# One chunk of the recurrent tail per step: reordering scans, square roots and first convolutions in a hybrid RG-LRU and attention kernel

## The chip, the cores and the metric

The kernel runs on one core of a Trainium2 chip. The metric is the device time of one execution in microseconds (us), the median of several runs; lower is better.

The engines are named as the profile names them: PE is TensorE's matrix multiply and PEld its weight load, DVE is VectorE, ACT is ScalarE, POOL is GpSimd, and SP is SyncE, whose queue issues nearly all transfers. Every engine works through its own queue strictly in order, so an instruction that waits holds everything behind it on the same engine.

## The reference

One layer of a hybrid decoder is computed for a prompt of 2048 tokens and for 64 sample tokens (8 sequences of 8): a recurrent branch, a dilated sliding-window attention over three groups of heads, and a gated merge of the two. The change touches the recurrent branch alone:

```
xa, ga = the first two blocks of 1024 columns of  rms_norm(x) @ w_in
xa = conv_b + sum(xa[t - 3 + j] * conv_w[j] for j in range(4))   # causal convolution
r  = sigmoid(xa @ w_a + b_a)       # block diagonal, 8 blocks of 128 channels
i  = sigmoid(xa @ w_x + b_x)
log_a = -8 * r * softplus(-lambda)
a  = exp(log_a)
u  = sqrt(-expm1(2 * log_a)) * (i * xa)
h[t] = a[t] * h[t-1] + u[t]        # the scan over time
out  = h * silu(ga)                # later multiplied by w_lru_proj
```

The kernel takes `-expm1(2 log_a)` as `(a*a + 1) * tanh(-log_a)`, so it needs a tanh, an exp, a square root and, for the gates and silu, sigmoids.

## The kernel before

All 2112 tokens (2048 of the prompt and 64 of the sample) lie along the free dimension, and the normalized, transposed input stays in SBUF as a high and a low part (`RH`, `RL`). Products are formed in three passes (high by high, high by low, low by high). The order of every engine is written out by hand (`tc.manual_schedule()`), so the program order of the Python code is the order on each engine's queue. The tokens are cut into five chunks, `CH`: 512, 512, 384, 384 and 320 tokens.

The program goes through attention and its gating, then the recurrent branch, which the change touches, then the merge gates (`gm_block`, with the sample attention planned into their steps), and then three output projections.

The recurrent branch loops over 8 blocks `b` of 128 channels. A block has two halves of five steps, one step a chunk:

- In the first half each step forms `xa` for one chunk with 24 matmuls (`zT`, L760) into a PSUM tile `zt` of which there are four, and `evac` (L861) copies it into `xpad`.
- In the second half each step forms `ga` for one chunk with 24 matmuls, puts silu of it into `sgl` (L961 on ACT, L962 on DVE), and then `gates_b` runs the six gate matmuls of that chunk (`zga`, L888), two sigmoids (`rr` L890, `ii` L892) and a product on POOL (L893). The gate matmuls read `xh`, the convolution's result split by `gates_a` into a high part (L879 on ACT) and a low part (L880 on DVE). `xh` is a single buffer. The third of the six gate matmuls is the first that reads the low part.
- `conv` for a chunk is an Identity on ACT (L868), then three multiply-adds on DVE (L870). It writes `xc`, which the tail of the block before still reads until its scan of that chunk is done.

What remains of a block after its gates, its tail, runs under the next block's matmuls: `tail_1` (tanh, L897), `tail_2` (exp on ACT L902, a square on POOL L904, a multiply-add on DVE L905), and `tail_3`: a square root on ACT (L910), a product (L911), the scan (L919) on DVE, the product with `sgl` on POOL (L920), and a store of `sgl` to `Y1` from SP's queue (L921). For block `b - 1` the steps of block `b` issue them so: `tail_1` in step 0, `tail_2` in step 1, `tail_3` of chunks 0 to 2 in step 2, `conv` of chunk 0 in step 3, and in step 4 `gates_a` of chunk 0, `tail_3` of chunks 3 and 4, and `conv` of chunk 1. In the second half step `ci` issues `gates_b` of chunk `ci`, `gates_a` of chunk `ci + 1` and `conv` of chunk `ci + 2`. Block 0 has no tail before it; block 7's tail runs in the first `gm_block`.

Of the kernel before, what the change touches and what calls it, by code (L numbers as in the profile page):

```python
# [13 lines left out]
AF = mybir.ActivationFunctionType  # L14
# [17 lines left out]
CH = ((0, 512), (512, 512), (1024, 384), (1408, 384), (1792, 320))  # L32
# [10 lines left out]
def program(tc, I, O, C, upto=99, debug=False):  # L43
# [7 lines left out]
    PE, ACT, DVE, POOL = nc.tensor, nc.scalar, nc.vector, nc.gpsimd  # L51
# [36 lines left out]
    def ztile(*tags):  # L88
        zi[0] += 1
        return ps.tile([128, 512], F32, name="zt", tag=tags[zi[0] % len(tags)])  # L90
# [6 lines left out]
    for g in (0, 1, 2):  # L97
        n = (WIN[g] - 8) * 1024
# [7 lines left out]
    def copy(n=1):  # L106
        for _ in range(n):
            if copies:
                i = dma(*copies.pop())
                if not G.manual:  # L110
                    tc.keep_in_program_order(i)
# [424 lines left out]
    for i in range(N + 3):  # L536
# [125 lines left out]
        if N - 4 < i < N:  # L662
            for k in range(3):
                if wbr:
                    n = min(wbr)
# [12 lines left out]
    def w_raw(src, nk=8):  # L678
        wr = wzp.tile([128, nk, 128], F32, name="wzr", tag="wzr")
        dma(wr, src)  # L680
        return wr

    def w_split(wr, eng, nk=8):
        w = wzp.tile([128, 2, nk, 128], F32R, name="wz", tag="wz", bufs=2)
        split(w[:, 0], w[:, 1], wr, eng)
        return w

    def wcols(c0):
        return win[:, c0:c0 + 128].rearrange("(k p) c -> p k c", p=128)
# [67 lines left out]
    def zT(z, w, c0, n):  # L757
        for i in range(24):
            k, p = divmod(i, 3)
            PE.matmul(z[:, 0:n], w[:, (0, 1, 0)[p], k, :], (RH, RH, RL)[p][:, k, c0:c0 + n], start=(i == 0), stop=(i == 23))  # L760
# [68 lines left out]
    def par_prep():  # L829
        prt = ps.tile([128, 8, 42], F32, name="prt", tag="tr")  # L830
        for n in range(8):
            PE.transpose(prt[:, n, :], rows[:, n * 128:(n + 1) * 128], ident[0:42, 0:42])
        DVE.tensor_copy(par, prt)
        DVE.tensor_scalar(e_, lam, -1.0, None, ALU.mult)
        DVE.tensor_tensor(e_, e_, lam, ALU.min)
        ACT.activation(e_, e_, AF.Exp)
        DVE.tensor_scalar(y_, e_, 2.0, None, ALU.add)
        DVE.reciprocal(y_, y_)
        DVE.tensor_mul(y_, y_, e_)
        DVE.tensor_mul(q_, y_, y_)  # L840
        DVE.tensor_scalar(c8, q_, 2.0 / 19, 2.0 / 17, ALU.mult, ALU.add)
        for i in (15, 13, 11, 9, 7, 5, 3, 1):
            DVE.tensor_mul(c8, c8, q_)
            DVE.tensor_scalar(c8, c8, 2.0 / i, None, ALU.add)
        DVE.tensor_mul(c8, c8, y_)
        DVE.tensor_scalar(e_, lam, -1.0, 0.0, ALU.mult, ALU.max)
        DVE.tensor_add(c8, c8, e_)
        DVE.tensor_scalar(n8, c8, 8.0, None, ALU.mult)
        DVE.tensor_scalar(c8, c8, -8.0, None, ALU.mult)
# [5 lines left out]
    tt = lp.tile([128, NT], F32, name="tt")  # L855
# [3 lines left out]
    def evac(c0, n, z):  # L859
        npr = min(n, SEQ - c0)  # L860
        ACT.copy(xpad[:, 3 + c0:3 + c0 + npr], z[:, 0:npr])  # L861
        if npr < n:
            ACT.copy(xsp[:, :, 3:11], z[:, npr:n].rearrange("p (s t) -> p s t", t=8))
# [13 lines left out]
    def gates_a(c0, n):  # L877
        xh = lp.tile([128, 2, 512], F32R, name="xh", tag="xh")
        ACT.copy(xh[:, 0, 0:n], xc[:, c0:c0 + n])  # L879
        DVE.tensor_sub(xh[:, 1, 0:n], xc[:, c0:c0 + n], xh[:, 0, 0:n].bitcast(F32))  # L880
        return xh
# [13 lines left out]
    def tail_1(b):  # L895
        for c0, n in CH:
            ACT.activation(tt[:, c0:c0 + n], rr[:, c0:c0 + n], AF.Tanh, scale=n8[:, b:b + 1])  # L897

    def tail_2(b):
        for c0, n in CH:  # L900
            s = slice(c0, c0 + n)
            ACT.activation(rr[:, s], rr[:, s], AF.Exp, scale=c8[:, b:b + 1])  # L902
            a2 = lp.tile([128, 512], F32, name="a2", tag="ii", bufs=2)
            POOL.tensor_mul(a2[:, 0:n], rr[:, s], rr[:, s])  # L904
            DVE.scalar_tensor_tensor(tt[:, s], a2[:, 0:n], 1.0, tt[:, s], ALU.add, ALU.mult)  # L905

    def tail_3(b, i0=0, i1=5):
        for c0, n in CH[i0:i1]:
            s = slice(c0, c0 + n)
            ACT.activation(tt[:, s], tt[:, s], AF.Sqrt)  # L910
            DVE.tensor_mul(xc[:, s], xc[:, s], tt[:, s])  # L911
            if c0 + n == NT:
                a0 = rr[:, SEQ:NT:8]
                hh = lp.tile([128, 8], F32, name="hh", tag="hh")
                DVE.tensor_mul(hh, a0, par[:, b, 34:42])
                DVE.tensor_add(xc[:, SEQ:NT:8], xc[:, SEQ:NT:8], hh)
                DVE.memset(a0, 0.0)
            init = 0.0 if c0 == 0 else tt[:, c0 - 1:c0]
            DVE.tensor_tensor_scan(tt[:, s], rr[:, s], xc[:, s], init, ALU.mult, ALU.add)  # L919
            POOL.tensor_mul(sgl[:, s], sgl[:, s], tt[:, s])  # L920
            dma(Y1[b][:, s], sgl[:, s])  # L921
        if i1 < 5:
            return
        POOL.tensor_copy(par[:, b, 4:5], tt[:, SEQ - 1:SEQ])
        POOL.tensor_copy(par[:, b, 34:42], tt[:, SEQ + 7:NT:8])

    for b in range(8):
        for ci, (c0, n) in enumerate(CH):
            z = early.pop(ci, None) if b == 0 else None
            if z is None:  # L930
                z = ztile("z", "S")
                zT(z, wx, c0, n)
            evac(c0, n, z)
            copy()
            if ci == 0:
                gr = lp.tile([128, 2, 128], F32, name="gr", tag="gr")
                dma(gr[:, 0], I["lru_w_a"][0, b])
                dma(gr[:, 1], I["lru_w_x"][0, b])
                wga = w_split(wgr, DVE)
                wxr = w_raw(wcols((b + 1) * 128 if b < 7 else C_GM))  # L940
            if b == 0 and ci == 2:
                par_prep()
            if b and ci < 3:
                (tail_1, tail_2, lambda b: tail_3(b, 0, 3))[ci](b - 1)
            if ci == 3:
                POOL.tensor_copy(xsp[:, :, 0:3], par[:, b, 10:34].rearrange("p (s j) -> p s j", j=3))
                gw_ = lp.tile([128, 2, 2, 128], F32R, name="gw_", tag="gw_")
                split(gw_[:, 0], gw_[:, 1], gr, DVE)
                conv(b, *CH[0])
            if ci == 4:  # L950
                xh = gates_a(*CH[0])
                if b:
                    tail_3(b - 1, 3, 5)
                conv(b, *CH[1])
        for ci, (c0, n) in enumerate(CH):
            z = ztile("z", "S")
            zT(z, wga, c0, n)
            if ci == 0:
                wx = w_split(wxr, DVE)
                wgr = w_raw(wcols(1024 + (b + 1) * 128 if b < 7 else C_GM + 128))  # L960
            ACT.activation(sgl[:, c0:c0 + n], z[:, 0:n], AF.Sigmoid)  # L961
            DVE.tensor_mul(sgl[:, c0:c0 + n], z[:, 0:n], sgl[:, c0:c0 + n])  # L962
            gates_b(b, c0, n, xh, gw_)
            if ci < 4:
                xh = gates_a(*CH[ci + 1])
            if ci < 3:
                conv(b, *CH[ci + 2])
            copy()
        POOL.tensor_copy(par[:, b, 0:3], xpad[:, SEQ:SEQ + 3])
        POOL.tensor_copy(par[:, b, 10:34].rearrange("p (s j) -> p s j", j=3), xsp[:, :, 8:11])  # L970
# [15 lines left out]
    def gm_block(f, w, hooks, gtile):  # L986
        for ci, (c0, n) in enumerate(CH):
            z = ztile("z", "S")
            zT(z, w, c0, n)
            for h in hooks.get(ci, ()):  # L990
                h()
            gt = gtile()
            ACT.activation(gt[:, 0:n], z[:, 0:n], AF.Sigmoid, bias=par[:, f % 8, 8 + f // 8:9 + f // 8])  # L993
            dma(Gsc[f][:, c0:c0 + n], gt[:, 0:n])  # L994
            copy()
            if plan and f:
                for fn in plan.pop(0):
                    fn()

    plan = []  # L1000
    wm = {0: wx}

    def nextw(f):
        if f + 1 < 16:
            wm[f + 1] = w_split(G.wr, DVE)

    def nextr(f):
        if f + 2 < 16:
            G.wr = w_raw(wcols(C_GM + (f + 2) * 128))

    G.wr = wgr
    gm_block(0, wm[0], {0: (lambda: nextw(0), lambda: nextr(0), lambda: tail_1(7), lambda: tail_2(7)), 1: (lambda: tail_3(7),), 4: (states,)},
             lambda: lp.tile([128, 512], F32, name="gt0", tag="ii", bufs=2))
    lr.close()
    gts = ExitStack()
# [387 lines left out]
    for c in range(8):  # L1403
        for f in range(8):
            n = c * 8 + f
# [51 lines left out]
    for c in range(8):  # L1457
        c0, n = TC[c]
# [128 lines left out]
```

## Time and profile before

| | |
|---|---|
| median of 3 runs | 2606.82 us (2605.22 to 2612.3) |
| the profiled execution's own time | 2603.89 us |
| its span, first to last instruction | 2602.1 us |
| mean granted TensorE clock | 0.988 of full speed |
| busy share of the span: DVE, ACT, POOL | 60%, 42%, 21% |

The busy share of an engine is an average over stages of different kinds; what a change within one stage can bring is read from that stage's own waits. A timeline row gives the start, the duration, the engine, the line, the operation, the tiles, and in brackets the idle time of the engine just before it and what ended that idle time.

### The profile page before, as it was taken

Reading aid. Unit: us, or ns where it says so; the run is one execution under the profiler, and the core shown is the slowest. Engines: PE = TensorE matmul, PEld = TensorE weight load, DVE = VectorE, ACT = ScalarE, POOL = GpSimd, SP = SyncE. Lnnn points to the kernel's source line nnn. Section 1 sums busy time; section 2 is a strip of 40 time slices with the busy share of each in tenths; the row PEclk is TensorE's granted clock in tenths of the full one; section 3 lists DMA queues with packets and bytes.
Section 4 is the critical chain, followed back from the end, with each engine's and each line's share of the span. In section 5 each row is a group of like instructions: output and inputs, shape, how many; then the busy total and the mean of one; then the engine's idle time right before and its main releaser. Section 6 shows DMA issues by size and latency. Waiting matters only on the chain. (4 is left out here: it accounts for less than half of the span.)

```text
span 2602.1 us, 44722 instructions
## 1 busy us (share of the span) xinstructions
PE 2512.8 (97%) x15196; PEld 2351.1 (90%) x15196; DVE 1553.9 (60%) x4805; ACT 1080.6 (42%) x3327; POOL 553.3 (21%) x897
## 2 busy tenths in 40 slices
PE   8999999999999999999999998999998999999999
PEld 7999999999999999999988887888887999998988
DVE  6744686777776777557555666655775723432322
ACT  5534453443453443444455545544556621211110
POOL 4422322221221221223223333320000002200000
PEclk9999999999999999999999999999999999999999
DMA  5443564555554343247533333346555569633332
GB/s 150 108 136 95 145 180 138 163 154 151 154 149 118 105 120 111 78 131 235 182 111 134 105 107 117 105 140 197 186 174 171 169 181 345 206 120 116 118 117 68
DMA packets 311289, 376.73 MB, mean 145 GB/s; under 512 B 54915, under 2 KB 254927, under 8 KB 308221
## 3 DMA queue, kind: packets, MB, share of 16 engines
q1 hardware_dynamic: 297028, 356.31, 44.4%
q0 software_dynamic: 14032, 17.57, 2.5%
q8 instruction: 120, 1.97, 0.3%
q14 instruction: 109, 0.89, 0.1%
HBM read 293.55 MB, written 168.31 MB: 177 GB/s over the span
## 5 line engine op out<-in xcount | busy, mean ns | idle before, releaser
L336 PE MATMUL z<-w,RH 128*128 128x384 f32 (+1 forms) x3088 | 889.2, 349 | 4.9 <-POOL w L317 2.4
L760 PE MATMUL zt<-RH,wz 128*128 128x384 f32 (+2 forms) x2560 | 705.9, 359 | 10.5 <-ACT gt L993 9.7
L336 PEld LDWEIGHTS z<-w,RH 128*128 128x128 f32 (+1 forms) x3088 | 553.3, 188 | 14.7 <-POOL w L317 6.5
L760 PEld LDWEIGHTS zt<-RH,wz 128*128 128x128 f32 x2560 | 471.2, 192 | 57.2 <-ACT gt L993 11.0
L336 PE MATMUL z<-w,RL 128*128 128x384 f32 x1544 | 520.3, 337 | 0.1
L760 PE MATMUL zt<-RL,wz 128*128 128x384 f32 (+2 forms) x1280 | 456.8, 357 | 0.0
L336 PEld LDWEIGHTS z<-w,RL 128*128 128x128 f32 x1544 | 291.5, 189 | 0.7 <-DVE RL L94 0.5
L178 DVE CUSTOM_DVE_ANT_0 kjk<-kt,qs 128x128 bf16<-128x128 f32 x768 | 228.1, 297 | 67.5 <-DMA SA<-Dsc 20.4
L760 PEld LDWEIGHTS zt<-RL,wz 128*128 128x128 f32 x1280 | 244.7, 191 | 23.0
L408 ACT ACTIVATE P<-P,o 128x128 f32<-128x128 f32 (+1 forms) x192 | 88.9, 463 | 311.1 <-DVE o L407 311.1
L345 ACT ACTIVATE jk<-z 128x128 bf16<-128x128 f32 (+1 forms) x408 | 113.0, 277 | 237.0 <-PE trc L376 173.6
L94 DVE TENSOR_TENSOR KQ<-trc,KQ 128x256 fp32r<-128x256 f32 x192 | 81.4, 424 | 208.7 <-ACT KQ L93 208.7
L347 POOL TENSOR_SCALAR ss<-ss 128x2 f32<-128x2 f32 (+1 forms) x204 | 44.5, 218 | 714.2 <-ACT jk L345 679.4
L1465 PEld LDWEIGHTS zt<-y1t,w_wlo 128*128 128x128 f32 x1536 | 190.3, 191 | 0.6
L1465 PE MATMUL zt<-y1t,w_wlo 128*128 128x256 f32 (+1 forms) x1536 | 190.6, 286 | 0.0
L1497 PE MATMUL zt<-w_wo,mt 128*128 128x512 f32 x672 | 162.0, 395 | 0.0
L1497 PEld LDWEIGHTS zt<-w_wo,mt 128*128 128x128 f32 x672 | 126.0, 188 | 30.7
L348 POOL TENSOR_TENSOR rs<-ss,neghalf 128x2 f32<-128x2 f32 (+1 forms) x204 | 142.6, 699 | 17.0
L1150 ACT ACTIVATE v<-v,P 128x128 f32<-128x128 f32 x256 | 81.1, 391 | 76.4 <-DMA v<-in_cache_kv_w 60.7
L434 DVE TENSOR_REDUCE o<-op 128x128 f32<-128x256 f32 x192 | 80.6, 420 | 44.9 <-PE op L429 44.8
L1499 DVE TENSOR_TENSOR xr<-zt,xr 128x512 f32<-128x512 f32 (+1 forms) x34 | 23.5, 692 | 137.3 <-PE zt L1497 132.6
L93 ACT CAST mt<-g 128x256 fp32r<-128x256 f32 x72 | 27.1, 388 | 187.2 <-DVE g L1468 172.1
(292 smaller groups left out, 4273.3 us busy)
## 6 DMA issues: line engine op xcount, KB each, us to landing
out_kv_s<-in_cache_kv_w SPq DMA_DIRECT2D x176, 480.0 KB
xt<-in_x_prompt SPq DMA_DIRECT2D x48, 512.0 KB
wr<-in_w_in SPq DMA_DIRECT2D x96, 192.0 KB
kt<-in_cache_kv_w SPq DMA_DIRECT2D x128, 128.0 KB
wzr<-in_w_in SPq DMA_DIRECT2D x32, 512.0 KB
v<-in_cache_kv_w SPq DMA_DIRECT2D x128, 128.0 KB
Osc<-o SPq DMA_DIRECT2D x192, 65.0 KB
ot<-Osc SPq DMA_DIRECT2D x32, 390.0 KB
```

The source lines that it names most:

```text
L94: eng.tensor_sub(l, src, h.bitcast(F32))
L178: DVE.tensor_tensor_reduce(jk, kts[q.tile][:, c], qts[t][:, c], 1.0, 0.0, ALU.mult, ALU.add, q.SC[:, o:o + 1])
L336: PE.matmul(u.z[0:m, :], (RH, RL, RH)[p][:, k, u.cols], Wt[(u.g, u.h), k][:, (0, 0, 1)[p], :], start=(i == 0), stop=(i == 23))
L345: ACT.activation(jk[0:m, :], z[0:m, i * 128:(i + 1) * 128], AF.Square, accum_out=u.ss[0:m, i:i + 1])
L347: POOL.tensor_scalar(u.ss[0:m, :], u.ss[0:m, :], 1.0 / HD, EPS, ALU.mult, ALU.add)
L348: POOL.tensor_tensor(u.rs[0:m, :], u.ss[0:m, :], neghalf[0:m, :], ALU.pow)
L408: ACT.activation(u.P[:, 0:n], u.P[:, 0:n], AF.Exp, bias=u.o[:, 128:129], scale=-1.0, accum_out=u.o[:, 129:130])
L434: DVE.tensor_reduce(u.o[:, 0:128], u.op.rearrange("p a b -> p b a"), AX.X, ALU.add)
L760: PE.matmul(z[:, 0:n], w[:, (0, 1, 0)[p], k, :], (RH, RH, RL)[p][:, k, c0:c0 + n], start=(i == 0), stop=(i == 23))
L1150: ACT.activation(v2s[n][:, h], v2s[n][:, h], AF.Copy, scale=P2[:, h, n:n + 1])
L1465: PE.matmul(z[:, 0:n], wl[k][:, (0, 1, 0)[p], f, :], y1s[c * 8 + k][:, (0, 0, 1)[p], 0:n], start=(i == 0), stop=(i == 23))
L1497: PE.matmul(z[0:m, :], ms_[k][:, (0, 0, 384)[p] + o:(0, 0, 384)[p] + o + m], wo[k][:, (0, 1, 0)[p], e * 4:(e + 1) * 4, :].rearrange("p k c ...
```

## The change

The square roots leave `tail_3` for a step of their own, `tail_r`, all five in step 2 of the first half. `tail_3` then handles one chunk in each of five steps: chunks 0, 1 and 2 in steps 2, 3 and 4 of the first half, chunks 3 and 4 in steps 0 and 1 of the second. The new block's `conv` of chunk 0 and the split of its gate weights move from step 3 to step 2, behind the scan of chunk 0; `gates_a` of chunk 0 and `conv` of chunk 1 move from step 4 to step 3, behind the scan of chunk 1. Nothing is added to or taken from what is computed.

```
--- before.py
+++ after.py
@@ -904,10 +904,13 @@
             POOL.tensor_mul(a2[:, 0:n], rr[:, s], rr[:, s])
             DVE.scalar_tensor_tensor(tt[:, s], a2[:, 0:n], 1.0, tt[:, s], ALU.add, ALU.mult)
 
+    def tail_r(b):
+        for c0, n in CH:
+            ACT.activation(tt[:, c0:c0 + n], tt[:, c0:c0 + n], AF.Sqrt)
+
     def tail_3(b, i0=0, i1=5):
         for c0, n in CH[i0:i1]:
             s = slice(c0, c0 + n)
-            ACT.activation(tt[:, s], tt[:, s], AF.Sqrt)
             DVE.tensor_mul(xc[:, s], xc[:, s], tt[:, s])
             if c0 + n == NT:
                 a0 = rr[:, SEQ:NT:8]
@@ -941,16 +944,16 @@
             if b == 0 and ci == 2:
                 par_prep()
             if b and ci < 3:
-                (tail_1, tail_2, lambda b: tail_3(b, 0, 3))[ci](b - 1)
-            if ci == 3:
+                (tail_1, tail_2, tail_r)[ci](b - 1)
+            if b and ci > 1:
+                tail_3(b - 1, ci - 2, ci - 1)
+            if ci == 2:
                 POOL.tensor_copy(xsp[:, :, 0:3], par[:, b, 10:34].rearrange("p (s j) -> p s j", j=3))
                 gw_ = lp.tile([128, 2, 2, 128], F32R, name="gw_", tag="gw_")
                 split(gw_[:, 0], gw_[:, 1], gr, DVE)
                 conv(b, *CH[0])
-            if ci == 4:
+            if ci == 3:
                 xh = gates_a(*CH[0])
-                if b:
-                    tail_3(b - 1, 3, 5)
                 conv(b, *CH[1])
         for ci, (c0, n) in enumerate(CH):
             z = ztile("z", "S")
@@ -963,6 +966,8 @@
             gates_b(b, c0, n, xh, gw_)
             if ci < 4:
                 xh = gates_a(*CH[ci + 1])
+            if b and ci < 2:
+                tail_3(b - 1, ci + 3, ci + 4)
             if ci < 3:
                 conv(b, *CH[ci + 2])
             copy()
@@ -1009,7 +1014,7 @@
             G.wr = w_raw(wcols(C_GM + (f + 2) * 128))
 
     G.wr = wgr
-    gm_block(0, wm[0], {0: (lambda: nextw(0), lambda: nextr(0), lambda: tail_1(7), lambda: tail_2(7)), 1: (lambda: tail_3(7),), 4: (states,)},
+    gm_block(0, wm[0], {0: (lambda: nextw(0), lambda: nextr(0), lambda: tail_1(7), lambda: tail_2(7)), 1: (lambda: tail_r(7), lambda: tail_3(7),), 4: (states,)},
              lambda: lp.tile([128, 512], F32, name="gt0", tag="ii", bufs=2))
     lr.close()
     gts = ExitStack()
```

## Rows read from the trace of the kernel before

**Rows 1.** Page, part 1: busy time, share of the span, instructions.

```profile
PE 2512.8 (97%) x15196; PEld 2351.1 (90%) x15196; DVE 1553.9 (60%) x4805; ACT 1080.6 (42%) x3327; POOL 553.3 (21%) x897
```

**Rows 2.** PE's waits, recurrent branch: total us, times, longest.

```profile
PE zga L888 <- ACT xh L879: 22.5, 7, 3.2
PE zga L888 <- DVE xh L880: 8.4, 7, 1.8
```

**Rows 3.** Timeline of PE, blocks 1 and 2.

```profile
1329.92 2.36 PE L888 MATMUL zga<-xh,gw__17935 128*128 128x512 f32 x6 [3.21 <-ACT xh L879]
...
1356.59 0.63 PE L760 MATMUL zt<-RH,wz 128*128 128x512 f32 x2
...
1384.71 0.40 PE L760 MATMUL zt<-RL,wz 128*128 128x512 f32 x1
1388.32 2.67 PE L888 MATMUL zga<-xh,gw__18385 128*128 128x512 f32 x6 [3.21 <-ACT xh L879]
...
1399.14 1.19 PE L888 MATMUL zga<-xh,gw__18385 128*128 128x512 f32 x4 [1.36 <-DVE xh L880]
```

**Rows 4.** Timeline of PE, second half of block 0, start of block 1.

```profile
1274.99 1.56 PE L888 MATMUL zga<-xh,gw__17501 128*128 128x512 f32 x6
...
1292.76 1.21 PE L888 MATMUL zga<-xh,gw__17501 128*128 128x384 f32 x6
...
1298.20 0.63 PE L760 MATMUL zt<-RH,wz 128*128 128x512 f32 x2
```

**Rows 5.** Windows, block 2: length, five engines' busy us, PEclk, DMA share, GB/s.

```profile
1388.00:1390.00 2.00, 1.68 (x5) 1.06 (x6) 1.67 (x3) 2.00 (x5) 0.00 (x0) 0.81 0.64 261
1390.00:1392.00 2.00, 2.00 (x6) 1.58 (x5) 1.97 (x5) 1.98 (x2) 1.16 (x1) 0.50 0.00 0
...
1398.00:1400.00 2.00, 0.86 (x4) 0.73 (x5) 1.96 (x4) 0.33 (x1) 0.00 (x0) 1.00 0.39 111
```

**Rows 6.** Timeline of DVE, block 2.

```profile
1377.84 1.23 DVE L919 TENSOR_TENSOR_SCAN tt<-rr,xc 128x512 f32<-128x512 f32 x1
...
1379.69 2.21 DVE L919 TENSOR_TENSOR_SCAN tt<-rr,tt,xc 128x512 f32<-128x512 f32 x1
...
1384.55 3.06 DVE L870 SCALAR_TENSOR_TENSOR xc<-xpad,par,xc 128x512 f32<-128x512 f32 x3
1388.30 0.69 DVE L880 TENSOR_TENSOR xh<-xc,xh 128x512 fp32r<-128x512 f32 x1 [0.68 <-ACT xh L879]
1388.90 0.55 DVE L911 TENSOR_TENSOR xc<-xc,tt 128x384 f32<-128x384 f32 x1
1389.49 1.02 DVE L919 TENSOR_TENSOR_SCAN tt<-rr,tt,xc 128x384 f32<-128x384 f32 x1
...
1395.56 2.32 DVE L94 TENSOR_TENSOR wz<-wzr,wz 128x1024 fp32r<-128x1024 f32 x1
...
1402.77 1.91 DVE L870 SCALAR_TENSOR_TENSOR xc<-xpad,par,xc 128x384 f32<-128x384 f32 x3
```

**Rows 7.** Timeline of ACT, block 2.

```profile
1379.10 0.82 ACT L868 ACTIVATE xc<-xpad,par 128x512 f32<-128x512 f32 x1 [2.21 <-DVE tt L919]
...
1387.65 0.62 ACT L879 CAST xh<-xc 128x512 fp32r<-128x512 f32 x1 [7.35 <-DVE xc L870]
```

**Rows 8.** Timeline of POOL, block 2.

```profile
1379.15 1.66 POOL L920 TENSOR_TENSOR sgl<-sgl,tt 128x512 f32<-128x512 f32 x1 [2.47 <-DVE tt L919]
...
1401.14 1.29 POOL L893 TENSOR_TENSOR xc<-xc,ii 128x512 f32<-128x512 f32 x1 [4.33 <-ACT ii L892]
```

**Rows 9.** POOL's product at line 893, all blocks: duration ns min/median/max.

```profile
L893 POOL TENSOR_TENSOR xc<-xc,ii x40: 881/1018/1816, 1278.1 to 1707.9; 128x512 f32<-128x512 f32 x16, 128x384 f32<-128x384 f32 x16, 128x320 f32<-128x320 f32 x8
```

**Rows 10.** Groups of DVE by form, block 0: busy us, mean ns, idle before.

```profile
L870 DVE SCALAR_TENSOR_TENSOR xc<-xpad,par,xc 128x512 f32<-128x512 f32 x6 | 4.5, 751 | 0.2
```

**Rows 11.** Groups of ACT, whole span: busy us, mean ns, idle before.

```profile
L910 ACT ACT_TABLE_LOAD x8 | 10.3, 1283 | 0.1
```

**Rows 12.** Transfers that touch Y1 or Y2, whole span.

```profile
DMA to landing us min/median/max: 3.2/6.2/12.6
```

More of the change, by code (lines that the diff above doesn't have):

```diff
@@ L905, in tail_2, with tail_r @@
             DVE.scalar_tensor_tensor(tt[:, s], a2[:, 0:n], 1.0, tt[:, s], ALU.add, ALU.mult)
+    def tail_r(b):
+        for c0, n in CH:
+            ACT.activation(tt[:, c0:c0 + n], tt[:, c0:c0 + n], AF.Sqrt)
     def tail_3(b, i0=0, i1=5):
@@ L909, in tail_3 @@
             s = slice(c0, c0 + n)
-            ACT.activation(tt[:, s], tt[:, s], AF.Sqrt)
             DVE.tensor_mul(xc[:, s], xc[:, s], tt[:, s])
@@ L943, in program @@
             if b and ci < 3:
-                (tail_1, tail_2, lambda b: tail_3(b, 0, 3))[ci](b - 1)
-            if ci == 3:
+                (tail_1, tail_2, tail_r)[ci](b - 1)
+            if b and ci > 1:
+                tail_3(b - 1, ci - 2, ci - 1)
+            if ci == 2:
                 POOL.tensor_copy(xsp[:, :, 0:3], par[:, b, 10:34].rearrange("p (s j) -> p s j", j=3))
@@ L949, in program @@
                 conv(b, *CH[0])
-            if ci == 4:
+            if ci == 3:
                 xh = gates_a(*CH[0])
-                if b:
-                    tail_3(b - 1, 3, 5)
                 conv(b, *CH[1])
@@ L965, in program @@
                 xh = gates_a(*CH[ci + 1])
+            if b and ci < 2:
+                tail_3(b - 1, ci + 3, ci + 4)
             if ci < 3:
@@ L1011, in program @@
     G.wr = wgr
-    gm_block(0, wm[0], {0: (lambda: nextw(0), lambda: nextr(0), lambda: tail_1(7), lambda: tail_2(7)), 1: (lambda: tail_3(7),), 4: (states,)},
+    gm_block(0, wm[0], {0: (lambda: nextw(0), lambda: nextr(0), lambda: tail_1(7), lambda: tail_2(7)), 1: (lambda: tail_r(7), lambda: tail_3(7),), 4: (states,)},
              lambda: lp.tile([128, 512], F32, name="gt0", tag="ii", bufs=2))
```

## The prediction

> **What bounds the kernel now.** I read the page first: PE is busy for 97% of the span [rows 1], so little but PE's own idle time and its slow clock can be won, and work saved on ACT, DVE or POOL is worth nothing by itself. The next view is the waits of PE alone, over the recurrent branch. It has two large rows, both at the gate matmuls, both seven times: 22.5 us for the high part of `xh` and 8.4 us for the low part [rows 2]. Seven is the number of blocks that run a tail of a block before them (1 to 7).
>
> The timeline of PE then gives one block. The gates of block 1 start at 1329.92 and those of block 2 at 1388.32, a period of 58.40 us. PE finishes the first `ga` chunk at 1384.71 + 0.40 = 1385.11, stands for 3.21 us, and in the next step stands again for 1.36 us for the low part [rows 3]. Block 0, which has no tail beside it, shows the pace without these waits: from its first gate matmul to the next block's first matmul 1298.20 - 1274.99 = 23.21 us [rows 4], against 1356.59 - 1329.92 = 26.67 us in block 1 [rows 3]. From a block's first matmul to its first gates PE needs 1385.11 - 1356.59 = 28.52 us. An unhindered block would so take 28.52 + 23.21 = 51.73 us, and 58.40 - 51.73 = 6.67 us are lost in each of seven blocks, 46.7 us in all.
>
> Where the loss beyond the two idle times comes from is in the windows. After the long wait the granted clock is 0.81 and then 0.50 in two windows of 2 us, half of 2.4 GHz; around the second wait of 1.36 us it stays at 1.00 [rows 5]. The long wait is paid a second time by the clock behind it, the short one isn't.
>
> Why the long wait is there is read on DVE and ACT. ACT waits 7.35 us for the convolution before it can cast `xh` [rows 7], because on DVE the convolution of chunk 0 (1384.55) stands behind three scans of the old block [rows 6]. The Identity that begins it had been done since 1379.92 [rows 7].
>
> **The change part by part.** Times are from here on counted from the block's first matmul (1356.59 in block 2).
>
> *Square roots together.* Five follow each other in step 2, before 3 in one place and 2 in another. The trace has 8 table loads of 1283 ns at that line for 8 tails [rows 11], one a tail already, so no load goes. Two roots of about half a us each move ahead of the Identity of chunk 0, which waits for the scan of chunk 0 anyway: nothing.
>
> *Convolution of chunk 0 behind the first scan.* The scan ends at 1379.07, or 22.5 [rows 6]. The Identity takes 0.82 [rows 7], the three multiply-adds 2.25 uncontended (3 x 751 ns [rows 10]) or 3.06 beside a POOL product [rows 6]; POOL's product with `sgl` starts just there, so I take 3.06: the convolution is done at 26.4, the high part of `xh` (0.62 [rows 7]) at 27.05. PE comes for it at 28.52. The long wait goes, and with it the slow clock. The low part stands in DVE's queue behind the product and scan of chunk 1: about 0.7 (0.55 for 384 tokens, made longer by 512/384), then 1.23 if POOL is free (the first scan) or 2.21 beside POOL's product [rows 6, 8]. POOL has long finished by then, so 1.23; then 0.69. Following instructions overlap by some 0.09 (1388.30 + 0.69 against 1388.90 [rows 6]), so it is there at 28.85, and PE wants it two matmuls after 28.52, at 28.98. No wait, with 0.1 us to spare; with the scan at 2.21 it would be 0.85.
>
> *Evacuations behind the waiting Identities.* ACT's copies of chunks 3 and 4 now stand behind Identities that wait for scans (to about 23.3 and 29). Four `zt` tiles cover them: the matmuls that need these two back begin at about 37 and 42. Nothing, and some 12 us of lateness would be covered.
>
> *The second half.* Here the removed work is late next. In before, DVE ran without a pause from 1388.90 to 1402.77 + 1.91 = 1404.68, 15.78 us, for the rest of the tail, two convolutions and a part of the third, a weight split and three splits of `xh` [rows 6]. All of it stays between the first low part and the convolution that the fourth chunk's gates need, and the product and scan of chunk 2 come in: 0.55 + 1.02 = 1.57 [rows 6]. DVE also waits for the Identity of chunk 1, which waits for its scan: about 0.3. And POOL's products with `sgl` of chunks 1 and 2 now fall here, 1.29 + 1.02 [rows 8, 9]. How much of a POOL product DVE loses lies between nothing and all of it; the scan beside a 1.29 us product lost 0.98, the convolution 0.81 beside a smaller one [rows 6, 8 to 10], and nothing is lost while DVE itself waits for ACT. I take two thirds, 1.5. Sum: 15.78 + 1.57 + 0.3 + 1.5 = 19.15. The convolution for the fourth chunk ends at 28.85 + 19.15 = 48.0, and the low part of its `xh` about 1.0 later, at 49.0. PE without waits gets there at 28.52 + (1292.76 - 1274.99) = 46.29 [rows 4], and wants the low part 0.35 later, 46.64. PE waits 49.0 - 46.6 = 2.4 us in all, spread over the gates of the second to fourth chunk in pieces of about 1 us, like the one of 1.36 that left the clock at 1.00 [rows 3, 5]. Behind the fourth chunk DVE has time again.
>
> The Trainium skill, "SBUF — State Buffer", section "Who interferes with whom", states that a VectorE instruction with two SBUF inputs and a GpSimd one that reads SBUF exclude each other, and that the one issued first holds the other for its whole length. By it the two thirds would be the whole wherever they meet, the second rival below; the scan at 2.21 beside 1.23 agrees with it, and 15.78 us of DVE beside four such products neither show nor deny it.
>
> *The sum.* 6.67 - 2.4 = 4.3 us in each of seven blocks, 30 us. Nothing takes it back: the order is written by hand, what follows starts when PE gets there, and block 7's tail in the first `gm_block` issues the same instructions in the same order on each engine. The profiled execution would go from 2603.89 to 2574; it lay 2.9 below the median of the runs, so the median goes from 2606.8 to 2577.
>
> **Bounds of the second half.** Four POOL products lie in the stretch already (chunks 3 and 4 of `sgl`, chunks 0 and 1 of `xc`): 1.02 + 0.88 + 2 x 1.29 = 4.5 us [rows 8, 9], of which by the same two thirds 3.0 are in the 15.78. Below: no POOL product costs DVE anything. Then 15.78 - 3.0 + 1.87 = 14.65 is early enough for every gate, all 46.7 us are won, and the time is 2560. Above: every POOL product in the stretch is paid in full. The new ones cost 2.3 instead of 1.5, the old ones 1.5 more: 21.45, a wait of 4.7, 2.0 us a block won, 2593.
>
> **The rivals.**
> 1. *All waits go* (2560 to 2568). For it: block 0's pace [rows 4], and DVE is busy for only 60% of the span [rows 1]. Against it: DVE had no pause in the stretch that gets longer.
> 2. *DVE takes the place of ACT's wait in full*: POOL and DVE exclude each other, and the gates wait 4 to 5 us a block for low parts, up to the bound above or a little beyond. At 5 that is 6.67 - 5 = 1.7 us a block, 12 us, about 2595. For it: scan and convolution [rows 6, 8]. Against it: the convolution lost less than a whole product [rows 6, 9, 10], and the times at which DVE waits for ACT let POOL through.
> 3. *It does nothing* (2600 to 2612): as in 2, and the pieces come together in one long wait at the third or fourth gates, so that the clock falls again (26.67 - 23.21 - 1.36 = 2.1 us a block with all that goes with it).
> 4. *Slower, by the stores.* Each chunk of `sgl` is overwritten by the new block's sigmoid (L961, on ACT) once its store has landed. The store of chunk 1 is now issued at about 30.3 and its overwriting is due when PE ends the second `ga` chunk, at about 35.5: 5 us. Stores and loads of these tensors took 3.2 to 12.6 us to land [rows 12]. ACT has about 2 us before `xh` for the third gates is late, so up to 7 us nothing happens; at 12.6 PE waits over 5 us at the third gates and the clock falls: 5.3 + 1.1 + 2.1 = 8.5 lost for 6.67, 2619. It decides from a landing of about 11 us. Against it: the range is mostly that of loads four times as large, and nothing else is queued at that moment but one copy.
>
> **How the numbers follow.** Within 0.3% (8 us) a measurement can't tell a change from none. Forecast, 2568 to 2586: 0.53. All waits go: 0.15. DVE in full, 2586 to 2599: 0.21. Nothing: 0.06. Slower: 0.05. Faster by over 0.3% is the first three, 0.89; same 0.06; slower 0.05. The range reaches from 2562 into the third case, to 2595, and leaves out the bare end of the second, the top of the third and the last two, some 0.2 together. All cases but the last two have one sign, so one range serves.
>
> **What would show it.** In the profile after: no wait of 3 us for L879 at `zga`; a granted clock of 1.00 through the branch; a period of about 54 us between the first gates of blocks; waits for L880, or short ones for L879, of 1 to 3 us a block at the second to fourth chunk; scans of 512 tokens at 1.2 us and not 2.2; still one table load per tail at L910; DVE without a pause for about 19 us behind the first low part. The forecast is wrong if the waits at the later gates sum to over 4 us or to under 1, if the clock still falls, or if ACT's sigmoid at L961 waits for a transfer.

## The result, and the profile after

| | before | changed |
|---|---|---|
| median | 2608.60 us (2605.22 to 2612.3, 4 runs) | 2572.27 us (2570.03 to 2578.51, 4 runs) |
| profiled execution, its span | 2603.89, 2602.1 | 2570.03, 2568.3 |
| ratio, 95% interval | | 0.9872, 0.9857 to 0.9886 |

The changed kernel is 36 us faster by the medians and 33.9 by the profiled executions. The forecast was 2577, with a range of 2562 to 2595.

The waits of PE over the recurrent branch of the changed kernel answer to [rows 2]. Beside two single waits at the branch's ends, which both kernels have, one row is left of the two at the gate matmuls. It has the same seven blocks, 1.2 us each instead of 3.2.

```profile
PE zga L888 <- ACT xh L879: 8.5, 7, 1.2
PE hp L982 <- POOL par L928: 5.4, 1, 5.4
```

The gate matmuls line by line show when the gates of block 1 and of block 7 start: (1647.1 - 1325.3) / 6 = 53.6 us a block, where it was 58.40 [rows 3].

```profile
L888 PE MATMUL zga<-xh,gw__17902 x30: 307/350/499, 1325.3 to 1350.4; 128*128 128x512 f32 x12, 128*128 128x384 f32 x12, 128*128 128x320 f32 x6
...
L888 PE MATMUL zga<-xh,gw__20602 x30: 307/352/503, 1647.1 to 1672.1; 128*128 128x512 f32 x12, 128*128 128x384 f32 x12, 128*128 128x320 f32 x6
```

Seven blocks at 58.40 - 53.63 = 4.77 us make 33.4 of the 33.9 us between the two profiled executions. The timeline of PE in block 2, which starts at 1350.58, answers to [rows 3, 4]: the first gates follow at once, the second are a little drawn out (six matmuls in 1.80 instead of 1.57), the third wait 1.22 us (the row shows the first four of their six matmuls).

```profile
1350.58 0.62 PE L760 MATMUL zt<-RH,wz 128*128 128x512 f32 x2
...
1378.93 1.57 PE L888 MATMUL zga<-xh,gw__18352 128*128 128x512 f32 x6
...
1385.93 1.80 PE L888 MATMUL zga<-xh,gw__18352 128*128 128x512 f32 x6
1393.12 1.21 PE L888 MATMUL zga<-xh,gw__18352 128*128 128x384 f32 x4 [1.22 <-ACT xh L879]
...
1398.68 1.41 PE L888 MATMUL zga<-xh,gw__18352 128*128 128x384 f32 x6
```

In the windows of 2 us the granted clock is 1.00 everywhere in the block, at the third gates too, where [rows 5] had 0.81 and 0.50 behind the long wait.

```profile
1390.00:1392.00 2.00, 1.90 (x11) 1.58 (x10) 1.96 (x2) 0.00 (x0) 2.00 (x2) 1.00 0.28 98
1392.00:1394.00 2.00, 0.88 (x4) 0.58 (x4) 1.97 (x5) 1.44 (x3) 0.06 (x1) 1.00 0.83 246
1394.00:1396.00 2.00, 2.00 (x13) 2.00 (x13) 1.90 (x7) 1.22 (x3) 0.62 (x1) 1.00 0.00 0
```

DVE's timeline in the same block answers to [rows 6]. The convolution of chunk 0 starts behind one scan, 5.0 us before the first gates of the block; the scan of chunk 1 takes 1.28 and not 2.21. What grew is the product of chunk 3, 1.64 where it took 0.55, and the convolution of chunk 2, 3.45 where it took 1.92.

```profile
1371.83 1.22 DVE L922 TENSOR_TENSOR_SCAN tt<-rr,xc 128x512 f32<-128x512 f32 x1
...
1373.94 2.71 DVE L870 SCALAR_TENSOR_TENSOR xc<-xpad,par,xc 128x512 f32<-128x512 f32 x3 [0.57 <-ACT xc L868]
...
1377.29 1.28 DVE L922 TENSOR_TENSOR_SCAN tt<-rr,tt,xc 128x512 f32<-128x512 f32 x1
1378.49 0.67 DVE L880 TENSOR_TENSOR xh<-xc,xh 128x512 fp32r<-128x512 f32 x1
...
1383.86 1.20 DVE L94 TENSOR_TENSOR wz<-wzr,wz 128x1024 fp32r<-128x1024 f32 x1
...
1386.41 1.64 DVE L914 TENSOR_TENSOR xc<-xc,tt 128x384 f32<-128x384 f32 x1
...
1389.03 3.45 DVE L870 SCALAR_TENSOR_TENSOR xc<-xpad,par,xc 128x384 f32<-128x384 f32 x3
...
1395.21 2.40 DVE L870 SCALAR_TENSOR_TENSOR xc<-xpad,par,xc 128x384 f32<-128x384 f32 x3
```

POOL's timeline has a product beside each of the two; e2 below shows that those of line 893 cost 2.0 us of it.

```profile
1384.03 1.92 POOL L923 TENSOR_TENSOR sgl<-sgl,tt 128x384 f32<-128x384 f32 x1 [3.72 <-DVE tt L922]
1385.90 1.74 POOL L893 TENSOR_TENSOR xc<-xc,ii 128x512 f32<-128x512 f32 x1
1389.19 1.31 POOL L923 TENSOR_TENSOR sgl<-sgl,tt 128x384 f32<-128x384 f32 x1 [1.55 <-DVE tt L922]
1390.46 1.60 POOL L893 TENSOR_TENSOR xc<-xc,ii 128x512 f32<-128x512 f32 x1
```

### The profile page after: what moved, and what is told of

It reads as the page before. It is cut to its first block, busy times and chain, and to the rows that moved or that the text cites. A ratio compares the mean times of both kernels' runs of the same rounds, so it can differ in the third digit from the quotient of the medians.

```text
span 2568.3 us, 44715 instructions
## 1 busy us (share of the span) xinstructions
PE 2501.8 (97%) x15196; PEld 2341.9 (91%) x15196; DVE 1541.6 (60%) x4805; ACT 1082.9 (42%) x3327; POOL 561.5 (22%) x897
## 3 DMA queue, kind: packets, MB, share of 16 engines
q8 instruction: 120, 1.97, 0.3%
```

## The experiments

Two questions were open. What are the 53.6 - 51.7 = 1.9 us a block that are still lost, and which part of the change, and of the loss before it, is worth what? Medians below are of 4 or more runs each; ratios are against the kernel before, run beside them. The intervals of e1 to e4 and of e6 overlap that of the changed kernel (0.9857 to 0.9886), so for a difference from it the traces speak: from the first gates of block 1 to those of block 7 the period is 53.6 us a block in the changed kernel, 53.45 in e1, 53.05 in e2 and e3, and 54.9 in e4 and e6.

**e1, the convolution ahead of the scan.**

```
             gates_b(b, c0, n, xh, gw_)
             if ci < 4:
                 xh = gates_a(*CH[ci + 1])
-            if b and ci < 2:
-                tail_3(b - 1, ci + 3, ci + 4)
             if ci < 3:
                 conv(b, *CH[ci + 2])
+            if b and ci < 2:
+                tail_3(b - 1, ci + 3, ci + 4)
```

> Changed kernel, but in the second half each step's convolution stands ahead of the scan instead of behind it. Theory (the 1.9 us a block that are left come from DVE's queue ahead of the third and fourth gates): product and scan of chunk 3 leave the way of the third gates, those of chunk 4 the way of the fourth; the wait of 1.2 us for the high part goes, the period falls from 53.6 to about 52.3 us, the time from 2572 to about 2563. Rival (DVE's whole work in the stretch counts, whatever its order): the wait moves to the fourth gates, time within 4 us of 2572.

Measured: 2571.28 us, ratio 0.9861 (0.9846 to 0.9877). The wait for the high part is gone, as the theory had it, but the time hardly moved: the rival was nearer. The split of the low part stands behind the same convolution and scan in DVE's queue, so the gates from the second chunk on now each wait a little for it: in PE's timeline of block 2 the third and fourth gates pause at their third matmul, and the fifth are drawn out to 1.38 from 1.04.

```profile
1388.79 0.51 PE L888 MATMUL zga<-xh,gw__18352 128*128 128x384 f32 x2
1389.49 0.96 PE L888 MATMUL zga<-xh,gw__18352 128*128 128x384 f32 x4 [0.20 <-DVE xh L880]
1394.46 0.51 PE L888 MATMUL zga<-xh,gw__18352 128*128 128x384 f32 x2
1395.36 0.96 PE L888 MATMUL zga<-xh,gw__18352 128*128 128x384 f32 x4 [0.39 <-DVE xh L880]
1399.81 1.38 PE L888 MATMUL zga<-xh,gw__18352 128*128 128x320 f32 x6
```

**e2, POOL's products at the end of the block.**

```
-        ii = lp.tile([128, 512], F32, name="ii", tag="ii", bufs=2)
-        ACT.activation(ii[:, 0:n], zs[1][:, 0:n], AF.Sigmoid, bias=par[:, b, 6:7])
-        POOL.tensor_mul(xc[:, c0:c0 + n], xc[:, c0:c0 + n], ii[:, 0:n])
+        ACT.activation(tt[:, c0:c0 + n], zs[1][:, 0:n], AF.Sigmoid, bias=par[:, b, 6:7])
...
             copy()
+        for c0, n in CH:
+            POOL.tensor_mul(xc[:, c0:c0 + n], xc[:, c0:c0 + n], tt[:, c0:c0 + n])
```

> Changed kernel, but POOL's five products of the convolution with the input gate stand together at the end of the block, where DVE is idle, instead of one behind each step's gates; the gate waits in tt until then. Theory (POOL's products hold DVE's two-operand instructions up): the product of chunk 3 falls from 1.64 to about 0.55 us, the convolution of chunk 2 from 3.45 to 2.3 or less, the wait at the third gates goes, time about 2563. Rival (DVE is merely full, POOL costs it little): DVE's durations fall by under 0.5 us a block, time within 3 us of 2572.

Measured: 2567.42 us, ratio 0.9848 (0.9833 to 0.9864). On DVE nearly the theory's numbers came: the product of chunk 3 takes 0.54, the convolution of chunk 2 takes 2.54 (2.3 or less was expected). The time gave back only half of the 9 us: POOL's late products begin as soon as POOL is free, run into the last convolution, and the fifth gates wait 0.65 us.

```profile
1385.46 0.54 DVE L912 TENSOR_TENSOR xc<-xc,tt 128x384 f32<-128x384 f32 x1
...
1386.97 2.54 DVE L870 SCALAR_TENSOR_TENSOR xc<-xpad,par,xc 128x384 f32<-128x384 f32 x3
...
1396.15 3.82 DVE L870 SCALAR_TENSOR_TENSOR xc<-xpad,par,xc 128x256 f32<-128x256 f32 x3
```

Two products of 1.29 us left the stretch of DVE between the first low part and the convolution for the fourth gates. In the changed kernel that stretch ran from 1378.49 + 0.67 to 1395.21 + 2.40, 18.45 us; here from 1377.53 + 0.67 to 1392.26 + 2.40, 16.46. So 2.58 us of POOL's work cost DVE 1.99, or 77%: 1.10 at the product of chunk 3 and 0.91 at the convolution of chunk 2.

**e3, both edits.** The two diffs above together.

> Both edits of e1 and e2. Theory: nothing holds PE at the gates any more, the period is that of block 0, 51.7 us, and the time 2572 - 13 = 2559. Rival (the second gates' low part still comes late, or ACT with its waits is next): period 52.2 or more, time 2563 or more.

Measured: 2568.30 us, ratio 0.9850 (0.9834 to 0.9867), no better than e2 alone, with the same period. The second, third and fourth gates are free, and the fifth wait 0.8 us behind a last convolution of 3.50 + 2.32 us beside POOL's late products. The time is in the rival's range, for a reason that neither named.

**e5, the late products held until the last gates.** In-order queues do the holding: with the last chunk's product in front, the four others stand behind it.

```
-        for c0, n in CH:
+        for c0, n in CH[4:] + CH[:4]:
             POOL.tensor_mul(xc[:, c0:c0 + n], xc[:, c0:c0 + n], tt[:, c0:c0 + n])
```

> e3, but of POOL's five late products that of the last chunk stands first, so that all of them wait for the block's last gates. In e3 the last convolution of a block took 3.50 + 2.32 us beside these products, and the fifth gates came 1.0 us late. Theory (POOL beside DVE again): that convolution falls to 1.5 + 0.9 us, the wait at the fifth gates goes, the period falls from 53.05 to about 52.0 us and the time by 7 us, to about 2561. Rival (the fifth gates are late for DVE's amount of work): period 52.8 or more, time within 3 us of e3.

Measured: 2561.27 us, ratio 0.9821 (0.9806 to 0.9835), below the interval of the changed kernel, 11 us by the medians. It and e10, whose interval overlaps, are the fastest kernels here. The last convolution takes 1.51 + 0.92, the gate matmuls have no wait in any block, and the period is (1635.0 - 1324.3) / 6 = 51.8 us, the pace of block 0. In a window from just before block 1's first gates to past block 7's last, PE is busy for all of it; the late products run where DVE has nothing to do:

```profile
1320.00:1680.00 360.00, 360.00 (x1878) 326.03 (x1877) 228.40 (x342) 215.55 (x367) 131.35 (x139) 1.00 0.39 129
```

```profile
1400.38 5.35 POOL L973 TENSOR_TENSOR xc<-xc,tt 128x320 f32<-128x320 f32 x5 [6.61 <-ACT tt L891]
1406.79 1.23 DVE L94 TENSOR_TENSOR wz<-wzr,wz 128x1024 fp32r<-128x1024 f32 x1 [6.94 <-ACT wz L93]
```

Whether the held products would do as much without e1's reordering was not run.

**e10, e5 with block 7's products left at their gates.** The line below stands in `gates_b`, and the late loop leaves block 7 out.

```
+        if b == 7:
+            POOL.tensor_mul(xc[:, c0:c0 + n], xc[:, c0:c0 + n], tt[:, c0:c0 + n])
...
-        for c0, n in CH[4:] + CH[:4]:
+        for c0, n in CH[4:] + CH[:4] if b < 7 else ():
```

> e5, but in block 7, whose tail starts at once in the first merge-gate block, POOL's products stay with their gates. In e5 PE waits 9.1 us for POOL's last copies of the states, against 5.4 in the changed kernel. Theory (the late products of block 7 hold its tail up by some 4 us): the wait returns to about 5.4, time 2561 - 3 to 4 = 2558. Rival (something else in that stage ends last): within 1.5 us of e5's 2561.3.

Measured: 2563.93 us, ratio 0.9828 (0.9815 to 0.9842). The wait for POOL's copies fell from 9.1 to 5.3 as expected, but in PE's timeline block 7's gates, beside POOL's products again, take 25.1 us from the first to the end of the last (1636.04 to 1661.15), where they took 23.6 in e5 (1634.97 to 1658.56). From block 7's first gates to the last transpose of the states that leaves 54.0 us instead of 56.3, and of these 2.3 us the times show nothing; what ends last behind them stays open. Neither the theory's time nor the rival's came.

**e4, the roots back at their scans.**

```
     def tail_3(b, i0=0, i1=5):
         for c0, n in CH[i0:i1]:
             s = slice(c0, c0 + n)
+            ACT.activation(tt[:, s], tt[:, s], AF.Sqrt)
...
-            if b and ci < 3:
-                (tail_1, tail_2, tail_r)[ci](b - 1)
+            if b and ci < 2:
+                (tail_1, tail_2)[ci](b - 1)
```

> Changed kernel, but each square root stands again right ahead of its chunk's product and scan, two of them so between the sigmoids of the second half. The prediction gave the gathering of the roots no value. Theory: four more table loads a block (1.28 us each, 28 in all) stand on ACT, of which its waits hide most; the root of chunk 4 and with it the fourth gates come 0.8 to 1 us later: 2572 + 6 = 2578. Rival (the gathering is what lets the scans spread): ACT becomes late at every gate, 3 us or more a block, 2593 or more. Rival of none: within 2 us of 2572.

Measured: 2577.97 us, ratio 0.9894 (0.9876 to 0.9913), the theory's number. Two groups of ACT show the price, at the sigmoid and at the root, 22 loads each where both had 8:

```profile
L965 ACT ACT_TABLE_LOAD x22 | 28.2, 1283 | 0.4
L914 ACT ACT_TABLE_LOAD x22 | 28.2, 1283 | 0.4
```

In the old order the roots stood together as far as table loads go [rows 11]. With scans spread between sigmoids they no longer would: the gathering is worth 5.7 us here by the medians, and the period, (1653.8 - 1324.5) / 6 = 54.9 us against 53.6, says the same. That it is worth nothing without the spreading follows from the count of loads alone; no run gathers the roots in the old order.

**e6, the scans' part alone.** The first convolutions and the first split go back to steps 3 and 4.

```
-            if ci == 2:
+            if ci == 3:
                 POOL.tensor_copy(xsp[:, :, 0:3], ...)
...
                 conv(b, *CH[0])
-            if ci == 3:
+            if ci == 4:
                 xh = gates_a(*CH[0])
                 conv(b, *CH[1])
```

> One part alone: roots together and scans one chunk a step as in the changed kernel, but the first two convolutions and the first split in steps 3 and 4 as before, so behind the scans of chunks 1 and 2. Theory (what counts is the sum of DVE's work ahead of each gate, and the scans of chunks 3 and 4 are out of the first gates' way): the first gates wait about 2 us, the later ones hardly; period within 0.6 us of the changed kernel's 53.6, time 2568 to 2577, clock 1.00. Rival (it is the convolutions' place ahead of the scans that wins): a wait of 3 us at the first gates, the clock falls behind it, 2590 or more.

Measured: 2577.00 us, ratio 0.9888 (0.9870 to 0.9905), at the upper edge of what the theory gave. The waits at the first gates are there, 1.08 us for the high part and 0.72 for the low, and the second to fifth gates have none. Not expected: in four of the seven blocks the clock fell behind them, as in PE's timeline and a window of block 2. There the period is 55.3 us, in block 3, where the clock stayed at full speed, 1490.0 - 1436.1 = 53.9, within the 0.6 us that the theory allowed. Here, where the later gates wait for nothing, the slow clock costs 1.4 us a block.

```profile
1380.74 0.73 PE L888 MATMUL zga<-xh,gw__18383 128*128 128x512 f32 x2 [1.08 <-ACT xh L879]
1382.19 2.04 PE L888 MATMUL zga<-xh,gw__18383 128*128 128x512 f32 x4 [0.72 <-DVE xh L880]
```

```profile
1382.00:1384.00 2.00, 1.80 (x4) 1.46 (x5) 1.97 (x3) 1.97 (x3) 1.00 (x1) 0.56 0.07 24
```

**e7, the convolutions' part alone.**

```
-            if b and ci > 1:
-                tail_3(b - 1, ci - 2, ci - 1)
+            if b and ci == 2:
+                tail_3(b - 1, 0, 1)
             if ci == 2:
...
                 conv(b, *CH[0])
+                if b:
+                    tail_3(b - 1, 1, 3)
             if ci == 3:
                 xh = gates_a(*CH[0])
                 conv(b, *CH[1])
+            if b and ci == 4:
+                tail_3(b - 1, 3, 5)
...
-            if b and ci < 2:
-                tail_3(b - 1, ci + 3, ci + 4)
```

> The other part alone: the first two convolutions and the first split one step earlier, as in the changed kernel, but the scans of chunks 1 and 2 right behind the first convolution and those of chunks 3 and 4 in the last step of the first half. Theory: the low part for the first gates comes about 2 us late, that for the second, behind four scans and a weight split, about 2.7 us late again; 5 us and, if the clock falls, up to 7 us a block are lost, time 2596 to 2610. Rival (the convolutions' place wins): time 2580 or less.

Measured: 2595.74 us, ratio 0.9952 (0.9937 to 0.9967), just under the theory's range; its runs lie far apart (2587.3 to 2601.4), and the profiled one is the slowest of them. PE waits 26.4 us for the low part in fourteen pieces, up to 2.2 us.

```profile
PE zga L888 <- DVE xh L880: 26.4, 14, 2.2
```

With the roots gathered in both, the scans' part brings 30 us alone and the convolutions' part 11; together they bring 36.

**e8, the kernel before with its long wait filled.**

```
+            if b and ci == 0:
+                fz = ps.tile([128, 512], F32, name="fz", tag="tr")
+                for i in range(14):
+                    PE.matmul(fz, wga[:, 0, 0, :], RH[:, 0, 0:512], start=(i == 0), stop=(i == 13))
             gates_b(b, c0, n, xh, gw_)
```

> The kernel before, with 14 matmuls of 128x512 on data at hand, whose result nobody reads, put ahead of the first gates in blocks 1 to 7: PE works through the 3.2 us in which it stood. Theory (the long wait is paid a second time by the clock): granted clock 1.00 through the block, from the first gates to the next block 24.7 to 25 us instead of 26.67, the time 2607 - 12 to 14 = 2594. Rival (the rows behind the wait are slow for another reason, or the wait isn't covered): time 2604 or more.

Measured: 2615.63 us, ratio 1.0035 (1.0022 to 1.0049): slower than before, and the theory fell. The clock did stay at 1.00 behind the filled wait. But then PE stood at the second gates, 0.68 us for the high part and 1.97 for the low, and behind that the clock fell for longer than it had.

```profile
1384.56 3.37 PE L966 MATMUL fz<-RH,wz 128*128 128x512 f32 x14
1387.95 1.93 PE L888 MATMUL zga<-xh,gw__18400 128*128 128x512 f32 x6
1396.07 0.73 PE L888 MATMUL zga<-xh,gw__18400 128*128 128x512 f32 x2 [0.68 <-ACT xh L879]
1398.78 2.08 PE L888 MATMUL zga<-xh,gw__18400 128*128 128x512 f32 x4 [1.97 <-DVE xh L880]
```

```profile
1400.00:1402.00 2.00, 2.00 (x7) 1.81 (x7) 1.16 (x2) 1.41 (x4) 0.35 (x1) 0.50 1.07 360
1402.00:1404.00 2.00, 2.00 (x8) 2.00 (x7) 1.96 (x3) 0.58 (x1) 0.93 (x1) 0.50 1.15 399
```

From the first gates to the low part of the second it is 1398.78 - 1387.95 = 10.83 us, with the clock at full speed; in the kernel before, with the clock at half for a part of it, 1399.14 - 1388.32 = 10.82 [rows 3]. That point is DVE's, whatever PE's clock is.

**e9, both waits filled.** The same with `ci < 2` and 11 matmuls ahead of the second gates.

> e8 with a second filling: 11 more matmuls of 128x512 ahead of the second gates, whose low part DVE delivers no earlier than in the kernel before (1398.72 after first gates at 1387.95 in e8, 1399.09 after 1388.32 before). Theory after e8 (the second gates wait for DVE whatever PE's clock is, so the slow clock behind the first wait cost the kernel before nothing; e8 lost time because its longer second wait slowed the clock behind it): granted clock 1.00 throughout, period 58.4 us as before, time 2602 to 2612. Rival (the slow clock costs what the prediction took for it, 1.7 to 2.1 us a block): 2596 or less. Rival (the added matmuls themselves cost): as e8, 2615 or more.

Measured: 2604.46 us, ratio 0.9988 (0.9979 to 0.9997), within 3 us of before. The clock is at 1.00 over whole blocks, PE is busy for 58.10 of 58.40 us, and the period is still 58.4:

```profile
1362.50:1420.90 58.40, 58.10 (x297) 51.44 (x296) 37.63 (x49) 30.70 (x54) 19.25 (x20) 1.00 0.35 124
```

So the slow clock cost the kernel before some 3 us by the medians, and 5.5 at the end of the interval, where the 1.7 to 2.1 us a block of the expectation would be 12 to 15. The 25 added matmuls a block did not lengthen the period.

## Why the prediction was right, point by point

**The loss and its place.** 6.67 us in each of seven blocks, all of it at the gates: right. e5, which takes every wait away, runs at 51.8 us a block against the 51.73 that block 0 promised.

**The first gates.** The low part of `xh` was forecast at 28.85 us from the block's first matmul; it is there at 1378.49 + 0.67 - 1350.58 = 28.6, and PE doesn't wait. The scan beside no POOL product was taken at 1.23 and took 1.28. The evacuations behind the Identities stand where the forecast put them (1373.81 and 1379.39, or 23.2 and 28.8 us), and PE has no wait for them.

**The second half.** DVE's stretch was forecast at 19.15 us and took 18.45; PE's residual wait at 2.4 and is 1.9 us a block. The gain came out at 4.8 instead of 4.3 us a block. The forecast spread the waits over the second to fourth gates in pieces of about 1 us; 1.2 of them stand at the third and the rest is small.

The size came so near by luck in part. Without the product and scan of chunk 2 (1.57) and the wait for the Identity (0.36), the stretch grew by 18.45 - 15.78 - 1.57 - 0.36 = 0.74 us, where the forecast had 1.5 for POOL's new products. The 0.74 is what is left of larger terms. New meetings with POOL added 1.09 at the product of chunk 3, 1.53 at the convolution of chunk 2 and 0.49 at that of chunk 3. Old ones went, which the forecast had carried along in its 15.78: the weight split fell from 2.32 [rows 6] to 1.20, the split of `xh` for the third gates from 1.29 to 0.56, and the small product `hh` from 0.97 to 0.16. In the kernel before:

```profile
1390.81 0.97 DVE L915 TENSOR_TENSOR hh<-rr,par 128x8 f32<-128x8 f32 x1
1399.01 1.92 DVE L870 SCALAR_TENSOR_TENSOR xc<-xpad,par,xc 128x384 f32<-128x384 f32 x3
1401.56 1.29 DVE L880 TENSOR_TENSOR xh<-xc,xh 128x384 fp32r<-128x384 f32 x1
```

```profile
1390.59 1.16 POOL L920 TENSOR_TENSOR sgl<-sgl,tt 128x384 f32<-128x384 f32 x1 [4.49 <-DVE tt L919]
1395.00 1.81 POOL L893 TENSOR_TENSOR xc<-xc,ii 128x512 f32<-128x512 f32 x1
```

The weight split meets a POOL product in both kernels; what changed is which of them began first. In the kernel before POOL's product of 1395.00 began ahead of the split of 1395.56, and the split took 2.32. In the changed one the split of 1383.86 began ahead of POOL's product of 1384.03, kept its 1.20, and the product took 1.92, where the one of 1390.59 had taken 1.16.

The share of a POOL product that DVE loses, taken at two thirds, measured 77% in e2. The rule of the Trainium skill that was weighed, "SBUF — State Buffer", section "Who interferes with whom", by which the later of two that meet is held for the whole of the earlier, fits single pairs nearly: the product of chunk 3 took 1.64 instead of 0.55 while POOL's product of 1385.90 ran, a loss of 1.09 us beside a product that takes 1.29 by itself. Where the remainder goes is not shown.

One reading in the forecast is off: between 1388.90 and 1404.68 DVE's rows hold three whole convolutions and two splits of `xh`, not two convolutions and a part of a third with three splits. The 15.78 us are right.

**The clock.** Here a step of the prediction failed: "the long wait is paid a second time by the clock behind it". e8 and e9 show that in the kernel before the slow clock lay in the shadow of the second gates, which waited for DVE anyhow: with the clock at 1.00 the period stayed at 58.4 us. The sum didn't suffer, since it used the whole 6.67 and not its parts. It would have misled whoever tried to win the clock alone.

**Square roots together at nothing** fits the count of loads in the old order and is wrong as a statement on this one: without it the spread scans cost 5.7 us (e4). It was costed as a move by itself, not as what another part of the change needs.

**The rivals.** All waits gone is what e5 reaches, by two more edits; DVE in ACT's place is there in part, 1.9 of the 4 to 5 us. Against the stores speaks the timeline of ACT: its sigmoid for chunk 1 starts at 1386.18, 0.09 us after PE's last matmul for that tile ends (1385.70 + 0.39), though the profile names an older release:

```profile
1386.18 0.60 ACT L964 ACTIVATE sgl<-zt 128x512 f32<-128x512 f32 x1 [1.19 <-POOL sgl L923]
```

In the kernel before the same gap is 0.08 (1397.32 to 1397.40). In all seven blocks of the changed kernel it is 0.08 or 0.09. No store held it.

## What to carry to other kernels

When an engine waits for another, sum the other's queue between two points at which the first must meet it, and compare that with the first one's own pace; here one such sum gave the gain within half a microsecond a block, and it is why filling the wait and saving the clock brought next to nothing in the kernel before. Where no later gate waits, the clock does cost time (e6). A wait that moves along when an instruction is moved (e1) belongs to the queue and not to the instruction in front. And helpers on a second engine should be put where the first is idle: holding five POOL products behind the last gates, by the order of POOL's queue alone, took 7 us off e3, where moving the convolutions ahead of the scans (e1) had taken off 1, which is within the noise.

## What the runs showed of the hardware that was not expected

The granted clock fell after split waits as well: in e6 behind 1.08 and 0.72 us with two matmuls between them, in four blocks and not in the other three, whereas 1.36 us [rows 5] and 1.22 us in one piece left it at 1.00 in the blocks shown. Added matmuls on idle stretches (25 a block in e9) kept it at 1.00 and left the period at 58.4 us.
